# The head of a one-core encoder step in another order: smaller first loads, no GpSimd low parts, forms built between the steps of the first root

## The chip, the cores and the metric

One core of a Trainium2 chip runs the whole kernel. The metric is device time in microseconds (us) of one execution. The engines are named as in the profile: PE (TensorE matmul), PEld (its weight loads), DVE (VectorE), ACT (ScalarE), POOL (GpSimd) and SP (SyncE, which here only issues transfers).

## The reference, cut to what matters

One layer works on 576 time steps (512 of one stream, 64 of another) with 1024 features:

```python
x = x + 0.5 * swiglu_ffn(rms_norm(x, ffn1_norm), ffn1_w_gate_up, ffn1_w_down)
h = rms_norm(x, mix_norm); p = h @ w_in      # two gated convolution branches follow
...
x = x + 0.5 * swiglu_ffn(rms_norm(x, ffn2_norm), ffn2_w_gate_up, ffn2_w_down)

def rms_norm(x, g):
    return x * rsqrt(mean(x * x, -1) + EPS) * g
def swiglu_ffn(x, w_gate_up, w_down):
    gate, up = split(x @ w_gate_up, 2, -1)
    return (silu(gate) * up) @ w_down
```

Only the start of the first of these lines, the norm and the first columns of `ffn1_w_gate_up`, is touched by the change. Everything is float32.

## The kernel before, in words

**Numbers in two parts.** Features lie on the 128 partitions, the 576 steps in the free dimension, so x is eight tiles x0 to x7. A float32 product is made of three matmuls: each operand is a high part (a copy rounded to `fp32r`) and a low part (the rest), and high times high, high times low and low times high are added up in PSUM, for two halves of 288 columns, so six matmuls for each tile of 128 rows. The high part is always a copy on ACT (CAST, or ACTIVATE with a scale). The low part comes in one of three ways: a subtraction on DVE; a subtraction on POOL; or "by DMA", where ACT writes the negated high part and POOL issues a transfer that adds the source onto it (DMA_DIRECT2D on POOL, with `accum_op=add`).

**Order.** Every compute engine keeps the order in which the Python code issues its instructions (`keep_in_program_order`), so an instruction that waits holds up all that stand behind it on its engine. SP issues all loads in order. Raw weights go through a ring of six buffers of 128 x 512 (`wraw`, `RAWS = 6`): the seventh load waits until the first one has been used up, by its low part. `Stream.prep` does one weight unit: load, high part, low part; `weights()` does three units, one for each of the first three products (`FIRST`: gate column 0, up column 0, gate column 1).

**The head.** `load(j)` fetches x tile j, `begin(j)` makes its two parts scaled by the norm's gain (`split_scaled`: ACTIVATE on ACT, SCALAR_TENSOR_TENSOR on DVE), `squares(j)` squares it on ACT or POOL, and `ss.add(dve)` adds a square to the sum `acc`. The weights of the first three products come in units of 1, 3 and 4 tiles of 128 rows (`FIRST_KS`). PE takes the eight tiles one after the other, three products at a time (18 matmuls for a tile); before the eighth, `rstd` issues eight matmuls with a tile of ones that sum the squares over partitions. `rstd` then goes: DVE `a = sum/D + EPS`, ACT reciprocal root `r`, three DVE steps that refine it.

**Forms.** From column block 3 on, gate and up are computed together with seven products instead of eight (a Strassen-type scheme, `pair`). It needs sums of quarter tiles of scaled x, the forms. There are four pairs of x tiles, p = 0 to 3. `Forms.scale(p)` writes two scaled copies (`w<-x,gains`, ACT), `combine(p)` four DVE operations on halves (`tmp<-w`) into two tiles and their high parts on ACT, `split(p)` the two low parts, on DVE or (`by_dma=True`) by DMA.

**The first three column blocks** are plain: `plain(i)` issues the products gate i and up i, then

```python
            gate()      # DVE: t = gate * R;  ACT: t = Silu(t)
            forming()   # the next group of form steps of `todo`
            hidden()    # DVE: t = up * t;    ACT: high part of t
            parts()     # DVE: low part of t
            forming()
```

A product needs a PSUM tile of two banks, and there are four (`mmps`, `bufs=4`): gate 0, up 0, gate 1 and the sum of squares hold them first, then up 1, gate 2, up 2 and the first pair reuse them in that order. Up 1 therefore cannot start before DVE's `a`, gate 2 not before DVE's gate multiplication of block 0, up 2 not before the `hidden` multiplication of block 0, and the first pair not before the gate multiplication of block 1. In a row `tmp<-mm,r` is a gate multiplication and `tmp<-mm,tmp` (576 columns) a `hidden` one; `g`, `u` and `act` are tiles with high and low parts.

Of the kernel before, what the change touches and what calls it, by code (L numbers as in the profile page):

```python
# [43 lines left out]

HALVES = ((0, H), (H, T))
LATE_SPANS = (((0, 304),), ((304, T),))
FIRST_KS = (1, 3, 4)
WARM = 10


# [53 lines left out]
def tile_encoder_step(  # L104
# [7 lines left out]
    pe, dve, sca, pool = (  # L112
        Ordered(tc, e, c)
        for e, c in (
            (nc.tensor, pe_cost), (nc.vector, dve_cost), (nc.scalar, None), (nc.gpsimd, None)
        )
    )
# [12 lines left out]
    def nm(s):  # L130
        uid[0] += 1
        return f"{s}_{uid[0]}"

    def atile(dt=F32, n=T):
        return act.tile([P, T], dt, tag="act", name=nm("act"))[:, :n]
# [7 lines left out]
    def wtile(dt=F32, n=LB - HB):  # L143
        return conv.tile([P, LB - HB], dt, tag="w", name=nm("w"), bufs=6)[:, :n]

    def ttile(dt=F32):
        return tmp.tile([P, T], dt, tag="tmp", name=nm("tmp"))
# [16 lines left out]
    def half(ap, s):  # L164
        return ap[:, s * H : (s + 1) * H]
# [11 lines left out]
    X = [cpool.tile([P, T], F32, tag=f"x{j}", name=f"x{j}") for j in range(KT)]  # L177
# [15 lines left out]
    class Stream:  # L193
# [28 lines left out]
        def load(self, r):  # L222
            while len(self.loaded) <= r:
                ap, k = self.raws[len(self.loaded)]
                t = wraw.tile([P, KU, P], F32, tag="raw", name=nm("raw"))[:, :k, :]
                nc.sync.dma_start(t, ap)
                self.loaded.append(t)
# [16 lines left out]
        def add(self):  # L244

            _, k, _, _, sums = self.units[self.added]
            for name, ops in sums:
                v = wtile(n=k * P).rearrange("p (k n) -> p k n", n=P)
                a, b = (self.source(o) for o in ops)
                dve.tensor_tensor(v, a, b, op=ALU.add)  # L250
                self.sums[name] = v
            self.added += 1
            self.load_ahead()

        def begin(self):

            n = self.begun
            src, k, home, how, _ = self.units[n]
            v = self.source(src)
            make = {"u": utile, "g": gtile, "act": atile}[home]  # L260
            hi, lo = (make(F32R, k * P).rearrange("p (k n) -> p k n", n=P) for _ in range(2))
            sca.copy(hi, v)
            if how == "dma":

                sca.mul(lo, hi.bitcast(F32), -1.0)
                pool.dma_start(lo.bitcast(F32), v, accum_op=ALU.add)
            self.ready[n] = (hi, lo)
            self.begun += 1
            self.load_ahead()
# [93 lines left out]
    row = 0  # L363
    for k in FIRST_KS:
        for name in FIRST:
# [26 lines left out]
    def mm(ps, w, kk, xs, first, last, spans=HALVES):  # L392


        (whi, wlo), (xh, xl) = w, xs
        parts = ((whi, xh), (whi, xl), (wlo, xh))
        for n, s in SIX:
            if s < len(spans):
                (a, b), (i, e) = parts[n], spans[s]
                pe.matmul(  # L400
                    ps[:, s, : e - i], a[:, kk, :], b[:, i:e],
                    start=first and n == 0, stop=last and n == 2,
                )
# [59 lines left out]
    def high(v):  # L463
        hi = atile(F32R)
        sca.copy(hi, v)
        return hi
# [79 lines left out]
            n = spans[0][1] - spans[0][0]  # L546
            return p[:, :, :n] if len(spans) == 2 else p[:, 0, :n]

    def rstd(total, spans=HALVES):

        a, t = ttile(), ttile()
        r = rpool.tile([P, T], F32, tag="r", name=nm("r"), bufs=2)
        tot = total.total(spans)
        span = slice(spans[0][0], spans[-1][1])
        shaped = halves if len(spans) == 2 else (lambda v: v)
        a, t, y = a[:, span], t[:, span], r[:, span]
        dve.tensor_scalar(shaped(a), tot, 1.0 / D, EPS, op0=ALU.mult, op1=ALU.add)
        sca.activation(y, a, AF.Abs_reciprocal_sqrt)
        dve.scalar_tensor_tensor(t, y, -0.5, y, op0=ALU.mult, op1=ALU.mult)
        dve.tensor_tensor(t, t, a, op=ALU.mult)  # L560
        dve.scalar_tensor_tensor(y, t, 1.5, y, op0=ALU.add, op1=ALU.mult)
        return r


    class Forms:
# [9 lines left out]
                sca.activation(b, X[j], AF.Copy, scale=par(j, self.r_g))  # L575

        def combine(self, p):
            (b1, b2), (c, d) = self.b.pop(p), (ttile() for _ in range(2))
            for out, a, b, op in (
                (half(c, 0), half(b1, 0), half(b1, 1), ALU.subtract),  # L580
                (half(c, 1), half(b2, 1), half(c, 0), ALU.add),
                (half(d, 0), half(b1, 1), half(b2, 1), ALU.subtract),
                (half(d, 1), half(b2, 0), half(c, 1), ALU.subtract),
            ):
                dve.tensor_tensor(out, a, b, op=op)
            self.t[p] = [(v, high(v)) for v in (c, d)]

        def split(self, p, by_dma=False):
            self.parts[p] = [
# [12 lines left out]
            return first[:KU], t2, t1, t3, first[KU:], second[KU:], t4  # L602


    ss = Sum()
    xg = []
    def load(j):
# [5 lines left out]
    def weights(lo=dve):  # L613
        for _ in FIRST:
            ws.prep(lo)

    def squares(*js):
        for j in js:
            ss.square(X[j], pool if j in (0, 2, 4) else sca)

    load(0)
    begin(0)
    squares(0)
    weights()
    load(1)
    begin(1)
    weights()
    load(2)
    load(3)
    begin(2)  # L630
    begin(3)
    squares(1, 2)
    weights(pool)
    for j in range(4, KT):
        load(j)
    ss.add(dve)
    ss.add(dve)
    squares(3)
    begin(4)
    begin(5)  # L640
    ss.add(dve)
    squares(5, 4)
    ss.add(dve)
    ss.add(dve)
    begin(6)
    begin(7)
    squares(6, 7)
    ss.add(dve)
    ws.eager = True
    for _ in range(4):  # L650
        ws.prep()
    forms1 = Forms(R_N1)
    forms1.scale(0)
    forms1.scale(1)
    forms1.combine(0)
    nc.sync.dma_start(prm, prm_src[:, R_CA:, :])
    table(AF.Abs_reciprocal_sqrt)
    first = {name: psum2() for name in FIRST}
# [5 lines left out]
            firstw[name] += [(w, kk) for kk in range(ws.units[n][1])]  # L664
    for k in range(KT):
        if k == KT - 1:
            R1 = rstd(ss)
        for name in FIRST:
            w, kk = firstw[name][k]
            mm(first[name], w, kk, xg[k], k == 0, k == KT - 1)  # L670
# [2 lines left out]
    ps = product(name, xg)  # L673
    early[name] = ps


    def split_early(p):
        one.split(p, by_dma=True)

    def update(j, ps, R=None):  # L680

# [8 lines left out]
    def ffn(f, xg, sums, finish, forms, R=None, todo=()):  # L690
# [5 lines left out]
        def plain(i, hs):  # L696
# [4 lines left out]
            if R is None:  # L701
                R = rstd(sums)
# [105 lines left out]
    def finish1(g, hs):  # L808
        table(AF.Abs_reciprocal_sqrt)
        ps = both([("f1", "d", g, j) for j in range(2)], hs)  # L810
        for j in range(KT):
# [6 lines left out]
    one = forms1  # L818
    ffn(
        "f1", xg, ss, finish1, one, R1,  # L820
        (
            ((split_early, 0), (one.scale, 2), (one.combine, 1)),
            ((split_early, 1), (one.scale, 3), (one.combine, 2)),
            ((one.split, 2), (one.combine, 3)),
            ((one.split, 3),),
        ),
    )
    ss, xg = nss, nxg
# [92 lines left out]
    for j in range(KT):  # L921
        raw = j < RAW_J
        xs = xg if raw else xn
        product(("p", 4, j), xs, gate_b(j, raw))
        if R is None:
            R = rstd(ss)
        if raw:
            xn.extend(scaled(range(3 * j, min(KT, 3 * j + 3)), R))
        product(("p", 3, j), xs, value_b(j))
# [142 lines left out]
    ss = Sum()  # L1072
# [3 lines left out]
    for n, j in enumerate(IN_TURN):  # L1076
# [5 lines left out]
        p = n // 2  # L1082
# [114 lines left out]
```

## Time and profile before

| | us |
|---|---|
| runs, median (lowest to highest of 3) | 1302.98 (1302.82 to 1303.01) |
| the profiled execution's own time | 1303.07 |
| its span, first to last instruction | 1301.3 |
| PE busy in the span | 1286.3 (99%) |
| DVE, ACT, POOL busy | 892.0, 778.5, 400.5 |
| first matmul on data starts at | 5.29 |
| PE starts up 1, gate 2, up 2, first pair at | 29.06, 35.38, 41.70, 48.02 |

In a row of the timeline stand the start (us from the span's beginning), the time until its last instruction ends, the engine, the operation, what it writes and reads (`out<-in`, buffer numbers left out), the shape and the count; in brackets the idle time of the engine before it and what ended it. The granted PE clock was 0.998 over the span.

### The profile page before, as it was taken

How to read it: one execution, taken by the hardware profiler on the slowest of the kernel's cores; microseconds unless marked ns; L12 is line 12 of the kernel's file. 1: busy time of each engine (PE TensorE's matmuls, PEld its weight loads, DVE VectorE, ACT ScalarE, POOL GpSimd, SP SyncE). 2: the span in 40 equal slices, each digit the busy share in tenths (PEclk: the TensorE clock that was granted, in tenths of full speed). 3: DMA queues.
4: the chain of work that ended last, by engine and by line, in shares of the span. 5: the costliest groups of instructions: out<-in, count | busy, mean ns of one | idle time of the engine just before them, and what ended most of it. 6: DMA issues, size and time to landing. Idle time of an engine off the chain costs nothing.

```text
span 1301.3 us, 25714 instructions
## 1 busy us (share of the span) xinstructions
PE 1286.3 (99%) x9746; PEld 1282.5 (99%) x9746; DVE 892.0 (69%) x1460; ACT 778.5 (60%) x1374; POOL 400.5 (31%) x502
## 2 busy tenths in 40 slices
PE   9999999999999999999999999999999999999997
PEld 8999999999999999999999999999999999999996
DVE  6758758748945899888895260336967848847955
ACT  8755655645677655555554684457665655654664
POOL 4242332332242544322221322222142141241233
PEclk9999999999999999999999999999999999999999
DMA  9797787886798797877775978776687796796784
GB/s 245 141 189 160 148 185 157 165 192 147 152 195 182 167 216 173 175 166 170 172 168 125 199 158 178 154 166 142 138 169 165 162 192 149 163 206 136 161 178 107
DMA packets 290108, 218.40 MB, mean 168 GB/s; under 512 B 15680, under 2 KB 251200, under 8 KB 289984
## 3 DMA queue, kind: packets, MB, share of 16 engines
q0 software_dynamic: 60768, 100.30, 46.4%
q1 hardware_dynamic: 227488, 115.62, 31.4%
q8 instruction: 77, 1.26, 0.4%
q10 hardware_dynamic: 1728, 0.84, 0.2%
q14 instruction: 47, 0.39, 0.1%
HBM read 113.81 MB, written 2.62 MB: 89 GB/s over the span
## 4 chain that ended last, share of the span: by engine, by line
PE 90%; issue 4%; DMA 2%; ACT 1%; POOL 1%; DVE 1%; DVEq 0%; POOLq 0%; ACTq 0%; SPq 0%
PE mm L80 90%; DMA g<-raw 1%; DMA raw<-in_ffn_w_gate_up_dram 1%; POOL act L80 1%; DVE tmp L80 0%; ACT u L80 0%; DMA gains<-in_params_dram 0%; POOL g L80 0%; ACT tmp L80 0%; ACT g L80 0%; DVE acc L80 0%; ACT act L80 0%; DVE x L80 0%; DVE g L80 0%; POOL tmp L80 0%
## 5 line engine op out<-in xcount | busy, mean ns | idle before, releaser
L80 PE MATMUL mm<-act,u 128*128 128x288 f32 x4686 | 660.9, 294 | 0.7 <-DVE u L80 0.5
L80 PEld LDWEIGHTS mm<-act,u 128*128 128x128 f32 x4686 | 630.9, 188 | 1.2 <-DVE u L80 0.7
L80 PE MATMUL mm<-act,g 128*128 128x288 f32 x2766 | 398.6, 294 | 2.1 <-DMA g<-raw 2.0
L80 PEld LDWEIGHTS mm<-act,g 128*128 128x128 f32 x2766 | 376.5, 188 | 2.9 <-DMA g<-raw 2.8
L80 POOL DMA_DIRECT2D u<-raw x204 | 176.3, 864 | 550.4 <-ACT u L80 492.2
L80 PE MATMUL mm<-act,act 128*128 128x288 f32 (+2 forms) x2244 | 307.6, 293 | 1.4 <-DVE act L80 1.4
L80 PEld LDWEIGHTS mm<-act,act 128*128 128x128 f32 x2244 | 297.8, 188 | 2.4 <-DVE act L80 2.1
L80 POOL DMA_DIRECT2D g<-raw x124 | 108.6, 876 | 247.2 <-ACT g L80 188.2
L80 ACT CAST u<-raw 128x512 fp32r<-128x512 f32 (+2 forms) x204 | 117.1, 574 | 108.6 <-PE mm L80 76.5
L80 DVE SCALAR_TENSOR_TENSOR w<-g,prm,w 128x606 f32<-128x606 f32 x232 | 179.3, 844 | 1.4 <-ACT w L80 1.4
L80 DVE TENSOR_TENSOR tmp<-mm,tmp 128x288 f32<-128x288 f32 (+1 forms) x244 | 109.7, 458 | 72.9 <-PE mm L80 53.5
L80 ACT ACTIVATE u<-u 128x512 fp32r<-128x512 f32 (+2 forms) x204 | 121.1, 594 | 6.5
L80 POOL DMA_DIRECT2D act<-raw x90 | 78.9, 876 | 50.6 <-ACT act L80 49.5
L80 DVE SCALAR_TENSOR_TENSOR tmp<-mm,r 128x576 f32<-128x576 f32 x48 | 36.3, 757 | 78.0 <-PE mm L80 77.8
L80 ACT CAST g<-raw 128x512 fp32r<-128x512 f32 (+2 forms) x124 | 67.7, 546 | 35.3 <-DMA raw<-in_ffn_w_down_dram 14.7
L80 ACT CAST act<-tmp 128x576 fp32r<-128x576 f32 x84 | 56.2, 674 | 52.4 <-DVE tmp L80 51.6
L80 ACT CAST g<-w 128x512 fp32r<-128x512 f32 x80 | 49.6, 619 | 63.0 <-DVE w L80 56.6
L80 ACT CAST u<-w 128x512 fp32r<-128x512 f32 x80 | 49.5, 619 | 61.9 <-DVE w L80 55.7
L80 DVE TENSOR_TENSOR act<-tmp,act 128x576 fp32r<-128x576 f32 x80 | 59.3, 754 | 21.3 <-ACT act L80 19.8
L80 ACT ACTIVATE g<-g 128x512 fp32r<-128x512 f32 (+2 forms) x124 | 70.4, 568 | 3.9
L80 ACT CAST act<-raw 128x512 fp32r<-128x512 f32 (+2 forms) x99 | 57.6, 583 | 16.1 <-PE mm L80 11.0
L80 DVE TENSOR_TENSOR w<-raw,raw 128x512 f32<-128x512 f32 x80 | 54.8, 685 | 11.0 <-DMA raw<-in_ffn_w_gate_up_dram 11.0
(88 smaller groups left out, 814.1 us busy)
## 6 DMA issues: line engine op xcount, KB each, us to landing
raw<-in_ffn_w_gate_up_dram SPq DMA_DIRECT2D x173, 256.0 KB, 3.4
u<-raw POOLq DMA_DIRECT2D x145, 256.0 KB, 4.0
raw<-in_w_in_dram SPq DMA_DIRECT2D x112, 256.0 KB, 3.4
act<-raw POOLq DMA_DIRECT2D x80, 256.0 KB, 4.8
raw<-in_ffn_w_down_dram SPq DMA_DIRECT2D x96, 192.0 KB, 3.5
g<-raw POOLq DMA_DIRECT2D x65, 256.0 KB, 3.8
g<-raw POOLq DMA_DIRECT2D x43, 192.0 KB, 4.5
u<-raw POOLq DMA_DIRECT2D x43, 192.0 KB, 4.5
```

Source lines behind the costliest of these rows:

```text
L80: return self.tc.keep_in_program_order(fn(*args, **kwargs))
```

## The change

It has five parts. (1) The first weight units are 1, 1, 2 and 4 tiles instead of 1, 3 and 4. (2) The three low parts of the last unit are made by DVE instead of POOL; the square of x4 goes from POOL to ACT. (3) In the head's code the parts of x tiles (`begin`) are issued ahead of squares and additions. (4) `rstd` takes a function `meanwhile` that it calls behind the root on ACT: there the second form is added, and both forms 0 and 1 get their high parts and, by DMA, their low parts. Before, the form 0 was combined with its high parts ahead of the root, and the rest was done in `plain(0)`. (5) In `plain(0)` forms 2 and 3 are now done, with low parts by DMA; before, that was spread over `plain(0)` and `plain(1)`, and the low parts of 2 and 3 were DVE's.

```diff
-FIRST_KS = (1, 3, 4)
+FIRST_KS = (1, 1, 2, 4)
...
-    def rstd(total, spans=HALVES):
+    def rstd(total, spans=HALVES, meanwhile=None):
...
         sca.activation(y, a, AF.Abs_reciprocal_sqrt)
+        if meanwhile:
+            meanwhile()
         dve.scalar_tensor_tensor(t, y, -0.5, y, op0=ALU.mult, op1=ALU.mult)
...
         def combine(self, p):
+            self.add(p)
+            self.cast(p)
+
+        def add(self, p):
...
-            self.t[p] = [(v, high(v)) for v in (c, d)]
+            self.t[p] = c, d
+
+        def cast(self, p):
+            self.t[p] = [(v, high(v)) for v in self.t[p]]
...
+    def split_early(p):
+        forms1.split(p, by_dma=True)
...
-            ss.square(X[j], pool if j in (0, 2, 4) else sca)
+            ss.square(X[j], pool if j in (0, 2) else sca)
...
     load(2)
+    begin(2)
+    weights()
     load(3)
-    begin(2)
     begin(3)
-    squares(1, 2)
-    weights(pool)
+    weights()
     for j in range(4, KT):
         load(j)
-    ss.add(dve)
+    squares(1, 2)
+    begin(4)
     ss.add(dve)
     squares(3)
-    begin(4)
     begin(5)
-    ss.add(dve)
-    squares(5, 4)
     ss.add(dve)
     ss.add(dve)
     begin(6)
+    squares(4, 5)
     begin(7)
+    ss.add(dve)
     squares(6, 7)
+    ss.add(dve)
     ss.add(dve)
...
     forms1.scale(0)
+    forms1.add(0)
     forms1.scale(1)
-    forms1.combine(0)
...
         if k == KT - 1:
-            R1 = rstd(ss)
+            R1 = rstd(ss, meanwhile=lambda: (
+                forms1.add(1), forms1.cast(0), split_early(0), forms1.cast(1), split_early(1)
+            ))
...
-            ((split_early, 0), (one.scale, 2), (one.combine, 1)),
-            ((split_early, 1), (one.scale, 3), (one.combine, 2)),
-            ((one.split, 2), (one.combine, 3)),
-            ((one.split, 3),),
+            ((one.scale, 2), (one.combine, 2), (split_early, 2)),
+            ((one.scale, 3), (one.combine, 3), (split_early, 3)),
```

Three places of the built order matter below. The first is ACT between its last weight copy of the head (`act<-raw`) and the first copy for up 1 (`g<-raw`); `tmp<-x` are squares, `act<-x,gains` high parts of x tiles. Before:

```order
L80 CAST act_184<-raw_182 128x512
L80 ACTIVATE tmp_194<-x_91 128x576
L80 ACTIVATE act_196<-x_92,gains 128x576
L80 ACTIVATE act_200<-x_93,gains 128x576
L80 ACTIVATE tmp_205<-x_93 128x576
L80 ACTIVATE act_211<-x_94,gains 128x576
L80 ACTIVATE act_215<-x_95,gains 128x576
L80 ACTIVATE tmp_219<-x_94 128x576
L80 ACTIVATE tmp_221<-x_95 128x576
L80 CAST g_236<-raw_224 128x512
```

The same stretch of ACT now:

```order
L80 CAST act_198<-raw_196 128x512
L80 ACTIVATE tmp_206<-x_89 128x576
L80 ACTIVATE act_210<-x_92,gains 128x576
L80 ACTIVATE tmp_215<-x_91 128x576
L80 ACTIVATE act_217<-x_93,gains 128x576
L80 ACTIVATE act_223<-x_94,gains 128x576
L80 ACTIVATE tmp_227<-x_92 128x576
L80 ACTIVATE tmp_229<-x_93 128x576
L80 ACTIVATE act_231<-x_95,gains 128x576
L80 ACTIVATE tmp_236<-x_94 128x576
L80 ACTIVATE tmp_238<-x_95 128x576
L80 CAST g_254<-raw_242 128x512
```

Two more squares (x1, which stood ahead of this stretch, and x4, which was POOL's) are in it. The second place is ACT from the first scaled copies to the first unit of up 2 (`g_450` before, `g_490` now). Before:

```order
L80 ACTIVATE w_269<-x_93,gains 128x576
L80 CAST act_278<-tmp_272 128x576
L80 CAST act_280<-tmp_273 128x576
L80 ACT_TABLE_LOAD
L80 ACTIVATE table_283<-eps 128x1
L80 ACTIVATE r_416<-tmp_414 128x576
L80 CAST g_450<-raw_232 128x512
```

Now:

```order
L80 ACTIVATE w_293<-x_93,gains 128x576
L80 ACT_TABLE_LOAD
L80 ACTIVATE table_297<-eps 128x1
L80 ACTIVATE r_430<-tmp_428 128x576
L80 CAST act_444<-tmp_286 128x576
L80 CAST act_446<-tmp_287 128x576
L80 ACTIVATE act_448<-act_444 128x576
L80 ACTIVATE act_451<-act_446 128x576
L80 CAST act_454<-tmp_438 128x576
L80 CAST act_456<-tmp_439 128x576
L80 ACTIVATE act_458<-act_454 128x576
L80 ACTIVATE act_461<-act_456 128x576
```

Behind the last of these stands `g_490`: two copies have gone from ahead of the root `r` to behind it, and eight form operations now stand between the root and the weights of up 2. The third place is DVE between the gate multiplication of block 0 (`tmp<-mm,r`) and the low part of its hidden tile (`act<-tmp,act`). Before:

```order
L80 TENSOR_TENSOR tmp_521<-mm_285,r_416 128x576
L80 TENSOR_TENSOR tmp_534<-w_268 128x288
L80 TENSOR_TENSOR tmp_534<-w_269,tmp_534 128x288
L80 TENSOR_TENSOR tmp_535<-w_268,w_269 128x288
L80 TENSOR_TENSOR tmp_535<-w_269,tmp_534 128x288
L80 TENSOR_TENSOR tmp_521<-mm_286,tmp_521 128x576
L80 TENSOR_TENSOR act_547<-tmp_521,act_545 128x576
```

Now:

```order
L80 TENSOR_TENSOR tmp_561<-mm_299,r_430 128x576
L80 TENSOR_TENSOR tmp_568<-w_564 128x288
L80 TENSOR_TENSOR tmp_568<-w_565,tmp_568 128x288
L80 TENSOR_TENSOR tmp_569<-w_564,w_565 128x288
L80 TENSOR_TENSOR tmp_569<-w_565,tmp_568 128x288
L80 TENSOR_TENSOR tmp_561<-mm_300,tmp_561 128x576
L80 TENSOR_TENSOR act_587<-tmp_561,act_585 128x576
```

The rows look alike, but the four form operations read other copies: `w_268` and `w_269` were written ahead of the root, `w_564` and `w_565` are written by ACT behind the Silu of block 0.

More of the change, by code (lines that the diff above doesn't have):

```diff
@@ L674, in tile_encoder_step @@
     early[name] = ps
-    def split_early(p):
-        one.split(p, by_dma=True)
     def update(j, ps, R=None):
```

## The prediction

> **What bounds the kernel now.** The page gives PE as 99% busy, so I read busy time by stretches first, to see where anything but PE can matter.
>
> ```profile
> 5.30:29.00 23.70, 22.26 (x154) 20.99 (x154) 18.06 (x25) 21.35 (x36) 11.53 (x9) 1.00 1.04 268
> 29.00:76.00 47.00, 44.31 (x329) 43.28 (x327) 35.19 (x63) 35.70 (x63) 15.34 (x18) 1.00 0.75 149
> 76.00:1301.00 1225.00, 1215.43 (x9250) 1213.91 (x9248) 838.31 (x1373) 718.72 (x1271) 372.09 (x469) 1.00 0.78 167
> ```
>
> The columns are the stretch, its length, and busy time (count) of PE, PEld, DVE, ACT and POOL, then clock, DMA share and GB/s. Behind 76 us PE is never short of work for long, and the change does nothing there; the question is only when PE gets through the first 62 us. In the first stretch ACT is busy 21.35 of 23.70 us, more than DVE: ACT is the scarce engine of the head. Next the timeline of PE: where does it stand still?
>
> ```profile
> 11.60 0.66 PE L80 MATMUL mm<-act,act 128*128 128x288 f32 x3 [0.62 <-DVE act L80]
> 22.39 1.87 PE L80 MATMUL mm<-act,act 128*128 128x288 f32 x12 [0.82 <-DVE act L80]
> ...
> 29.06 3.19 PE L80 MATMUL mm<-act,g 128*128 128x288 f32 x23
> 35.38 3.32 PE L80 MATMUL mm<-act,g 128*128 128x288 f32 x24
> 41.70 3.32 PE L80 MATMUL mm<-act,g 128*128 128x288 f32 x24
> 48.02 1.74 PE L80 MATMUL mm<-act,g 128*128 128x288 f32 x12
> 49.60 1.49 PE L80 MATMUL mm<-act,u 128*128 128x288 f32 x10
> ...
> 60.84 1.60 PE L80 MATMUL mm<-act,g 128*128 128x288 f32 x10 [1.51 <-DMA g<-raw]
> 62.28 1.75 PE L80 MATMUL mm<-act,u 128*128 128x288 f32 x12
> ...
> 75.36 3.71 PE L80 MATMUL mm<-act,g 128*128 128x288 f32 x26 [0.47 <-DMA g<-raw]
> ```
>
> A product takes 6.32 us (29.06 to 35.38), a unit of the first pair 1.58 (48.02 to 49.60). PE waits 1.44 us in the head, and longest at 60.84, for the low part of the pair's seventh unit, which comes by DMA. So a head that PE passes sooner is worth something only if that low part comes sooner too. The chain of waits names its last steps, and the timeline of ACT shows what they hang on:
>
> ```profile
> 57.50 3.30 DMA g<-raw
> ```
> ```profile
> 13.20 0.62 ACT L80 CAST act<-raw 128x512 fp32r<-128x512 f32 x1 [0.24 <-DMA raw<-in_ffn_w_gate_up_dram]
> ...
> 17.56 1.25 ACT L80 ACTIVATE tmp<-x 128x576 f32<-128x576 f32 x2
> 18.71 0.61 ACT L80 CAST g<-raw 128x512 fp32r<-128x512 f32 x1
> ...
> 23.41 2.76 ACT L80 ACTIVATE w<-x,gains 128x576 f32<-128x576 f32 x4
> 26.07 1.23 ACT L80 CAST act<-tmp 128x576 fp32r<-128x576 f32 x2
> 27.32 1.28 ACT L80 ACT_TABLE_LOAD   x1
> ...
> 35.07 0.69 ACT L80 ACTIVATE tmp<-tmp 128x576 f32<-128x576 f32 x1
> 35.66 1.24 ACT L80 ACTIVATE act<-act 128x576 fp32r<-128x576 f32 x2
> 36.81 1.43 ACT L80 ACTIVATE w<-x,gains 128x576 f32<-128x576 f32 x2
> 38.14 1.81 ACT L80 CAST act<-tmp 128x576 fp32r<-128x576 f32 x3
> 39.85 1.26 ACT L80 ACTIVATE act<-act 128x576 fp32r<-128x576 f32 x2
> ...
> 45.53 0.69 ACT L80 ACTIVATE tmp<-tmp 128x576 f32<-128x576 f32 x1 [0.82 <-DVE tmp L80]
> 47.73 2.08 ACT L80 CAST act<-tmp 128x576 fp32r<-128x576 f32 x3 [1.51 <-DVE tmp L80]
> ...
> 53.84 0.69 ACT L80 ACTIVATE tmp<-tmp 128x576 f32<-128x576 f32 x1
> ```
>
> The rows without brackets followed the one before them without a wait: from 13.20 on, where ACT last waits for a load of the head, it is full for 30 us. The Silus of blocks 0, 1 and 2 (`tmp<-tmp`) stand at 35.07, 45.53 and 53.84, and the wanted low part lands 6.95 us after the third. I cost the change along this chain, in three sections.
>
> **ACT from 13.20 to the first Silu.** Two squares more (x1 and x4): two take from 17.56 to 18.71, +1.15. Two form copies less ahead of the root: 26.07 to 27.32, -1.25. Eight form operations more behind the root: a copy costs 0.57 (three from 38.14 to 39.85), a negated one 0.58 (35.66 to 36.81), so +4.6. Nothing covers them, since ACT has no gap to put them in. Sum +4.5: the first Silu at 39.6.
>
> **First to second Silu.** Both now have 15 ACT operations between them, but the waits differ. The DVE rows for it, before:
>
> ```profile
> 44.74 0.75 DVE L80 TENSOR_TENSOR tmp<-mm,r 128x576 f32<-128x576 f32 x1
> ...
> 47.23 0.46 DVE L80 TENSOR_TENSOR tmp<-w,tmp 128x288 f32<-128x288 f32 x1
> ...
> 48.35 0.75 DVE L80 TENSOR_TENSOR tmp<-mm,tmp 128x576 f32<-128x576 f32 x1
> 49.84 2.10 DVE L80 TENSOR_TENSOR act<-tmp,act 128x576 fp32r<-128x576 f32 x3 [0.74 <-ACT act L80]
> 51.85 0.69 DVE L80 TENSOR_TENSOR u<-w,u 128x512 fp32r<-128x512 f32 x1
> 52.45 0.69 DVE L80 TENSOR_TENSOR w<-w,raw 128x512 f32<-128x512 f32 x1
> ```
>
> Silu at 39.6, 0.59 to the next operation, two scaled copies 1.43: 41.6. Only then can DVE do the last three form operations of p = 2 (47.23 to 48.35: 1.12) and the hidden multiplication behind them (0.75): 43.5. On ACT the second form's high part waits for the fourth form operation and ends at 43.5, two negated copies and the hidden high part (0.67) end at 45.2, two scaled copies at 46.6. DVE's three operations for p = 3 end at 47.8, then a high part, two negated copies and the g copy on ACT: 50.2; DVE's low part of g (0.6 until the next starts, as from 51.85 to 52.45) and the gate multiplication of block 1 (0.75): 51.6. The second Silu moves from 45.53 to 51.6, so this section is 12.0 instead of 10.46: +1.55.
>
> **Second to third Silu.** Here the change pays back: no forms and no form low parts stand in this section any more. Silu 0.69, hidden multiplication 0.75, its high part 0.67, its low part 0.67, the low part and sum of weights 0.6 each, gate multiplication 0.75, and 0.04 at four handovers: 4.9 instead of 8.31, -3.4. From there to the landing nothing changes, 6.95.
>
> **The sum:** 4.5 + 1.55 - 3.4 = +2.65. The low part lands at 63.45 instead of 60.79, the seventh unit ends as much later, and 1303.07 becomes 1305.7. That is against the profiled execution; the median of the runs is 0.09 lower, so I say 1305.6.
>
> **PE on the way.** Smaller loads, DVE low parts instead of these,
>
> ```profile
> 12.49 5.16 POOL L80 TENSOR_TENSOR act<-raw,act 128x512 fp32r<-128x512 f32 x3 [1.55 <-ACT act L80]
> ```
>
> and inputs ahead of squares can free at most the 1.44 us of head waits and the restarts beside them. But up 1 needs the bank that DVE's `a` frees, and `a` stands behind form 0, which needs the second scaled copy: 23.41 + 1.43 + 1.15 = 26.0, three form operations 1.2, `a` 0.75: 28.0 against 29.06, a gain of 1.1 at most. Gate 2 then starts at 34.3 and up 2 could at 40.6, but its bank is freed at 43.5: a new wait of 2.9 us. It ends at 49.8, and the first pair's bank is free at 51.6: another 1.8. The pair's seven units (11.06) then end at 62.65 without any further wait, at 64.9 with the late low part, against 62.28 now. So the head's gain is covered by a wait behind it, whatever its size: I cost parts 1 to 3 at nothing, as long as PE reaches up 2 before 43.5. The wait at 51.3 for DVE's low part of form 3 goes with that operation; what is late in its place is the bank. The four more form transfers on POOL's queue stand ahead of the last two g and u transfers, but POOL idles more than it works (15.34 of 47.00 us), so I take nothing; at most they crowd the last landing, whose median over the kernel is longer than the 3.30 here:
>
> ```profile
> g<-raw POOLq DMA_DIRECT2D x65, 256.0 KB, 3.8
> ```
>
> That bounds it at 0.5 us more; below 3.3 I see none. The wait at 75.36 (0.47 and a restart) moves along, since ACT, DVE and PE shift alike; if it is absorbed, 0.7 comes back.
>
> **The start of the chain.** Where ACT's 13.20 goes is not shown before: the third load of the four-tile unit is issued later. Before, the three were issued one behind the other from 5.87:
>
> ```profile
> 5.87 1.48 SPq L226 DMA_DIRECT2D raw<-in_ffn_w_gate_up_dram  x3
> ```
> ```profile
> 7.16 0.82 DVE L80 SCALAR_TENSOR_TENSOR act<-x,gains,act 128x576 fp32r<-128x576 f32 x1 [0.92 <-ACT act L80]
> ```
>
> Now their buffers are those of tile 1's unit, freed by the DVE low parts that follow x1's (the second row) from 7.9 on, so SP issues the third at about 9.2 instead of 6.9. From issue to landing the loads took:
>
> ```profile
> DMA to landing us min/median/max: 2.7/3.7/4.1
> ```
> ```profile
> DMA to landing us min/median/max: 5.5/6.0/6.3
> ```
>
> The first row is of the six loads up to 5 us, the second of the three after it, in a full queue. So it lands between 11.9 and 15.5, and ACT can be held up by +2.3; below, the copies of x3 and the two loads ahead of it keep ACT busy until about 12.6, so -0.6. I take no shift: the DMA share of 1.04 says the engines move bytes without pause in this stretch, and the bytes ahead of this load are the same as before. The Trainium skill ("DMA: Bandwidth & Descriptors", section "Bandwidth") speaks against the smaller loads: it gives 0.95 us of transfer for 64 KB and 6.15 for 1 MB, and advises batches of 1 MiB. By its table, interpolated, three loads of 64 and three of 128 KB take about 6.7 us where three of 192 KB take 4.9; an estimate by that page would put the sum at 1307.4. The rows before show loads overlapping, so I give that no more than the rival below.
>
> **Rivals.** (a) *The chain starts sooner.* If ACT's load comes 0.6 earlier and the wait at 75.36 is absorbed as well, 2.65 falls to 1.35: 1304.3, not slower by what can be told. From 0.1 us saved on it decides, since 0.2% is 2.6. For it: nothing ties the load to 13.20. Against: the same bytes precede it, and both savings are needed for the full amount. Chance 0.22. (b) *The smaller loads arrive late:* ACT starts up to 2.3 us later and each microsecond goes to the end, 1307 in the middle, 1308 at most. Against it stands the full DMA share. Chance 0.13. (c) *The head's gain stays:* up 1's 1.1 us with all other waits unchanged gives 1301.9, and with the pair's wait of 1.5 gone too 1300.4. It needs the first Silu by about 36.7 (2.9 earlier than I put it), so ACT would have to hide five of the eight operations; the rows show no gap. Chance 0.08. (d) *All is covered, no change,* 1303: the four low parts that DVE drops (2.7 us) would have to shorten the chain by 2.65 more than I count in the third section, where I already let two of them go. Chance 0.05. My forecast, 1305.6 with 1304.9 to 1306.4 as its own range, has 0.52.
>
> **Numbers.** A measurement here tells 0.2% (2.6 us) from no change. Slower by more: a little over half of my forecast, 0.3, and nearly all of (b): 0.42. Faster by more is half of (c): 0.04. Same: 0.54. The range 1302.5 to 1307.2 leaves out (c) and the far half of (b), and 0.05 around them.
>
> **What would show it.** After: PE waiting about 3 us before up 2 (near 43) and about 1.8 before the pair (near 51), each for a DVE `tmp`; the Silus near 39.6, 51.6 and 56.5; the seventh unit's low part landing near 63.4; no wait for DVE's `act` in the pair. I am wrong if ACT has a gap between 13 and 40, if its start at 13.20 moves by over 0.6, or if a PE wait of the pair is set by another landing.

## The result, and the profile after

The changed kernel takes 1307.63 us (median of 6 runs, 1306.55 to 1308.62) beside 1302.93 us for the kernel before on the same chip. The ratio is 1.0035, with a 95% interval of 1.0024 to 1.0045: slower by 0.35%, about 4.7 us, where +2.6 was forecast. The profiled execution took 1307.66 us with a span of 1305.9, 4.6 longer than before.

Where the time goes is read in the same order as before. First the stretches (length, busy time of PE, PEld, DVE, ACT and POOL with counts, clock, DMA share, GB/s):

```profile
5.30:29.00 23.70, 22.49 (x154) 21.28 (x153) 16.85 (x31) 20.06 (x36) 4.74 (x5) 1.00 0.94 244
29.00:76.00 47.00, 41.39 (x303) 40.27 (x304) 30.77 (x56) 38.73 (x68) 16.71 (x20) 1.00 0.85 171
76.00:1301.00 1225.00, 1218.71 (x9273) 1216.74 (x9272) 839.24 (x1376) 719.41 (x1275) 375.62 (x471) 1.00 0.79 167
```

The loss is in the second row: PE got through 303 matmuls from 29 to 76 us, against 329 before. ACT has become busier there (38.73 us, 35.70 before). The first row holds something unforecast: the DMA share fell from 1.04 to 0.94. Next, the rows of PE's timeline in which it stood still:

```profile
29.30 3.40 PE L80 MATMUL mm<-act,g 128*128 128x288 f32 x24 [0.47 <-DVE tmp L80]
36.30 3.46 PE L80 MATMUL mm<-act,g 128*128 128x288 f32 x24 [0.43 <-DVE tmp L80]
44.69 3.36 PE L80 MATMUL mm<-act,g 128*128 128x288 f32 x24 [1.70 <-ACT act L80]
52.91 1.82 PE L80 MATMUL mm<-act,g 128*128 128x288 f32 x12 [1.75 <-DVE tmp L80]
60.30 1.59 PE L80 MATMUL mm<-act,g 128*128 128x288 f32 x10 [0.55 <-DMA g<-raw]
64.64 1.60 PE L80 MATMUL mm<-act,g 128*128 128x288 f32 x10 [0.88 <-DMA g<-raw]
```

The two forecast waits are there, 1.70 us before up 2 and 1.75 before the first pair, and the pair still ends on its seventh unit, whose low part comes by DMA. The row at 44.69 names ACT, but the forecast cause fits: DVE's multiplication that frees the bank of up 2 ends at 44.54 (43.79 + 0.75).

```profile
43.79 0.75 DVE L80 TENSOR_TENSOR tmp<-mm,tmp 128x576 f32<-128x576 f32 x1
```

The old wait at 51.3 for a low part by DVE is gone. The wait of 0.55 us at 60.30 is new: it is for an earlier low part of the pair, also by DMA, and one of the signs that the prediction named for being wrong. Up 1 starts at 29.30, no sooner than before (29.06). Last, the chain on ACT, and the chain of waits where it ends:

```profile
12.77 0.62 ACT L80 CAST act<-raw 128x512 fp32r<-128x512 f32 x1 [0.39 <-DMA raw<-in_ffn_w_gate_up_dram]
13.65 0.62 ACT L80 CAST act<-raw 128x512 fp32r<-128x512 f32 x1 [0.26 <-DMA raw<-in_ffn_w_gate_up_dram]
14.47 0.62 ACT L80 CAST act<-raw 128x512 fp32r<-128x512 f32 x1 [0.20 <-DMA raw<-in_ffn_w_gate_up_dram]
...
40.62 0.69 ACT L80 ACTIVATE tmp<-tmp 128x576 f32<-128x576 f32 x1
...
52.80 0.68 ACT L80 ACTIVATE tmp<-tmp 128x576 f32<-128x576 f32 x1 [0.91 <-DVE tmp L80]
...
57.68 0.69 ACT L80 ACTIVATE tmp<-tmp 128x576 f32<-128x576 f32 x1
```
```profile
61.34 3.26 DMA g<-raw
```

The last weight copy of the head starts at 14.47 instead of 13.20, the Silus at 40.62, 52.80 and 57.68, and the low part lands at 64.60 (61.34 + 3.26) instead of 60.79: 3.81 us later. Of this lag 0.35 us is made up by 143 us (PE is 3.46 behind there); about 0.25 is lost near 346 us and 0.56 near 942, and the last matmul starts 4.27 later than before. The last 0.3 us of the span come behind it.

### The profile page after: what moved, and what is told of

It reads as the page before. It is cut to its first block, busy times and chain, and to the rows that moved or that the text cites. A ratio compares the mean times of both kernels' runs of the same rounds, so it can differ in the third digit from the quotient of the medians.

```text
span 1305.9 us, 25749 instructions
## 1 busy us (share of the span) xinstructions
PE 1286.9 (99%) x9746; PEld 1282.6 (98%) x9746; DVE 888.0 (68%) x1462; ACT 780.9 (60%) x1382; POOL 398.7 (31%) x502
## 3 DMA queue, kind: packets, MB, share of 16 engines
q8 instruction: 77, 1.26, 0.4%
## 4 chain that ended last, share of the span: by engine, by line
PE 89%; issue 4%; ACT 3%; DMA 2%; DVE 1%; POOL 0%; SPq 0%; DVEq 0%; POOLq 0%; ACTq 0%
PE mm L80 89%; DMA g<-raw 1%; ACT act L80 1%; DVE tmp L80 1%; DMA raw<-in_ffn_w_gate_up_dram 1%; ACT u L80 1%; ACT tmp L80 1%; ACT g L80 0%; ACT w L80 0%; DVE acc L80 0%; SPq L226 0%; POOL g L80 0%; DVE x L80 0%; DVE g L80 0%; POOL act L80 0%
## 5 line engine op out<-in xcount | busy, mean ns | idle before, releaser
L80 DVE TENSOR_TENSOR act<-tmp,act 128x576 fp32r<-128x576 f32 x76 | 56.6, 754 | 19.7 <-ACT act L80 18.3
L80 ACT CAST act<-raw 128x512 fp32r<-128x512 f32 (+3 forms) x102 | 58.1, 571 | 16.5 <-PE mm L80 11.0
L80 DVE TENSOR_TENSOR w<-raw,raw 128x512 f32<-128x512 f32 x80 | 54.8, 686 | 12.1 <-DMA raw<-in_ffn_w_gate_up_dram 12.1
```

The lines of the kernel that those rows point to most:

```text
L80: return self.tc.keep_in_program_order(fn(*args, **kwargs))
```

## The experiments

Each kernel ran beside the kernel before on the same chip. "Copy" is the start of ACT's last weight copy of the head, "landing" that of the first pair's last low part, both from one profiled execution, while the median is of all runs; the share is that of the DMA engines from 5 to 11 us. Kernels are in the order of the landing.

| kernel | share | copy | landing | median us | ratio (95%) |
|---|---|---|---|---|---|
| e9: combination, root first | 0.99 | 13.12 | 59.83 | 1303.14 | 0.9999 to 1.0022 |
| before | 1.06 | 13.20 | 60.79 | 1303 | 1 |
| e7: head only, two squares on DVE | 1.02 | 13.01 | 60.84 | 1303.35 | 0.9994 to 1.0011 |
| e6: e7 and four low parts by DVE | 0.98 | 13.01 | 61.34 | 1304.80 | 1.0011 to 1.0038 |
| e10: before, small loads only | 0.87 | 13.75 | 61.58 | 1304.07 | 0.9999 to 1.0016 |
| e3: before, forms moved only | 1.04 | 13.07 | 62.12 | 1304.55 | 1.0001 to 1.0019 |
| e5: head only | 1.02 | 13.67 | 62.92 | 1305.03 | 1.0005 to 1.0023 |
| e1: after, units of 1, 3, 4 | 1.04 | 13.17 | 63.24 | 1305.39 | 1.0011 to 1.0028 |
| e2: after, forms as before | 0.83 | 14.43 | 63.77 | 1305.70 | 1.0012 to 1.0030 |
| e4: after, own buffers | 0.90 | 13.69 | 63.80 | 1306.99 | 1.0018 to 1.0041 |
| e13: after, loads joined | 1.01 | 14.18 | 64.35 | 1306.08 | 1.0013 to 1.0031 |
| e16: e1, loads cut | 0.91 | 14.35 | 64.44 | 1306.58 | 1.0017 to 1.0039 |
| e12: after, x3 first, own buffers | 0.88 | 14.43 | 64.55 | 1306.72 | 1.0017 to 1.0039 |
| e11: after, x3 first | 0.89 | 14.45 | 64.59 | 1306.81 | 1.0017 to 1.0039 |
| after | 0.80 | 14.47 | 64.60 | 1307.63 | 1.0024 to 1.0045 |

Above 60.8 the time follows the landing roughly one to one (e4, e6 and the changed kernel itself are about 1 us above that); below it, in e9, it doesn't. The medians of e6 and e9 stand for two groups of times each, see the last section.

### One part alone, and one part undone

**e3**, only parts 4 and 5: the head and `FIRST_KS` are those before.

```diff
-FIRST_KS = (1, 1, 2, 4)
+FIRST_KS = (1, 3, 4)      # and load ... squares ... add of the head as before
```

> The kernel before with only the forms moved (parts 4 and 5 of the change); its head as before. Theory: ACT to the first Silu -1.25 + 4.6 = +3.35, to the second +1.55, to the third -3.4: the low part lands at 60.79 + 1.5 = 62.3, time 1304.5. Rival (the forms carry the whole loss): 1307.6. Rival (moving them is neutral, the loss is the head's): 1303.0.

Time 1304.55, landing 62.12, against 1304.5 and 62.3. From the copy at 13.07, the Silus stand at

```profile
38.19 0.69 ACT L80 ACTIVATE tmp<-tmp 128x576 f32<-128x576 f32 x1
50.31 0.68 ACT L80 ACTIVATE tmp<-tmp 128x576 f32<-128x576 f32 x1 [0.91 <-DVE tmp L80]
...
55.18 0.69 ACT L80 ACTIVATE tmp<-tmp 128x576 f32<-128x576 f32 x1
```

so the sections are 25.1, 12.1 and 4.9 us (before: 21.9, 10.5, 8.3), and the forms' share of the loss is 1.3 us at the landing. Neither rival holds: the forms alone are not the whole loss, and moving them isn't neutral.

**e2**, the forms put back and the head left changed:

```diff
+    forms1.combine(0)
...
-            R1 = rstd(ss, meanwhile=...)
+            R1 = rstd(ss)      # and todo of plain as before
```

> The changed kernel with the forms where they were before (form 0 ahead of the root, the rest in the plain blocks, low parts of forms 2 and 3 by DVE); the head as changed. Theory (one chain on ACT, every microsecond of the head goes through): the first Silu at 35.07 + 1.27 (late loads) + 1.15 (two squares) = 37.5, the low part lands at 60.79 + 2.4 = 63.2, time 1305.4. Rival (the forms carry the whole loss and the head's delay is taken up by waits): 1303.0 to 1303.5.

1305.70 and a landing at 63.77, 0.3 and 0.6 above the theory; the rival (1303.0 to 1303.5) is out. ACT's timeline shows the excess, a wait for the first raw load of the first pair (the third weight copy behind the root; up 2's two stand ahead of it), which the kernel before hardly had (0.14 us):

```profile
34.95 0.62 ACT L80 CAST g<-raw 128x512 fp32r<-128x512 f32 x1 [0.82 <-DMA raw<-in_ffn_w_gate_up_dram]
```

**e1**, the units back at 1, 3 and 4 tiles:

```diff
-FIRST_KS = (1, 1, 2, 4)
+FIRST_KS = (1, 3, 4)
     begin(2)
-    weights()
     load(3)
```

> The changed kernel with the weight units of the head back at 1, 3 and 4 tiles; all else as changed. Theory (the late start of ACT's chain is the smaller units' doing, worth 1.27 of the 3.81 us by which the pair's seventh low part lands later): ACT's last weight copy of the head starts near 13.2 instead of 14.47, the low part lands near 63.3 instead of 64.6, time near 1306.3. Rival (the order of loads and x parts in the head delays it, not the sizes): the copy stays near 14.4 and the time at 1307.6. Rival (the late loads explain the whole loss): 1303.

Copy at 13.17 and landing at 63.24, as the theory has it; the time came out at 1305.39, 0.9 below the theory. So the change without its small units still loses 2.4 us, and with them about 2.2 more in the medians, 1.36 of it at the landing.

**e10**, the small units alone on the kernel before:

```diff
-FIRST_KS = (1, 3, 4)
+FIRST_KS = (1, 1, 2, 4)
     begin(2)
+    weights()
     begin(3)
```

> The kernel before with only its weight units at 1, 1, 2 and 4 tiles (part 1 alone). Theory: the third four-tile load is issued near 9 and lands near 14.4, ACT's last weight copy starts 1.2 us later than in the kernel before, all later ACT work with it, so the last low part lands at 62.0 and the time is 1304.2. Rival (the late load costs only together with the new order of the head): 1303.0. Rival (an improvement, since smaller loads let PE start sooner): 1302.

1304.07 and a landing at 61.58, near the theory. But the copy started only 0.55 us later (13.75), not the 1.2 expected, though the third four-tile load was issued at 8.96, as expected. The interval (0.9999 to 1.0016) doesn't separate it from no change, and with 0.07% it is the smallest part. It isn't faster.

### Is the head's earlier pass worth anything?

**e5** keeps of the change only parts 2 and 3 (loads of 1, 3 and 4 tiles, forms as before); **e7** also moves the squares of x1 and x4 from ACT to DVE:

```diff
-            ss.square(X[j], pool if j in (0, 2) else sca)
+            ss.square(X[j], {0: pool, 1: dve, 2: pool, 4: dve}.get(j, sca))
```

> The changed kernel with loads of 1, 3 and 4 tiles and the forms where they were before: what is left of the change is the head's order, the low parts by DVE instead of GpSimd, and the squares of x1 and x4 on ACT behind the last weight copy. Theory (ACT's chain): chain starts near 13.2 as before, two squares more, so the low part lands at 60.79 + 1.15 = 61.9 and the time is 1304.1, although PE passes the head about 1 us sooner. Rival (PE's earlier head is worth something by itself): 1302.

> As the head-only kernel (loads of 1, 3 and 4 tiles, forms as before, low parts by DVE), with the squares of x1 and x4 on DVE instead of ACT. Theory: ACT's chain is as long as before, so the low part lands near 60.8 and the time is 1303.0, with PE's start of up 1 about 1 us earlier all the same and all of that lost again at the waits. Rival (the head's earlier pass counts): 1302. Rival (DVE now is late with the sum of squares): 1304.

e5 took 1305.03, 0.9 above the theory: its landing at 62.92 is +0.47 by a later copy, +1.15 by the squares, and about the rest a wait of 0.71 us (0.14 before) for the same raw load as in e2 (at 34.09). e7 took 1303.35, ratio 1.0003: no change. Its PE timeline is the clearest evidence of the study:

```profile
27.86 3.32 PE L80 MATMUL mm<-act,g 128*128 128x288 f32 x24
...
46.81 1.74 PE L80 MATMUL mm<-act,g 128*128 128x288 f32 x12
...
51.36 0.53 PE L80 MATMUL mm<-act,u 128*128 128x288 f32 x2 [1.48 <-DVE act L80]
...
60.89 1.60 PE L80 MATMUL mm<-act,g 128*128 128x288 f32 x10 [1.52 <-DMA g<-raw]
```

PE starts up 1 at 27.86 instead of 29.06 and is 1.21 us ahead at the first pair (46.81 against 48.02). At 51.36 it waits for DVE's low part of a form, 1.48 instead of 0.23 us, and at 60.89 it is 0.05 behind the kernel before. The whole 1.2 us is handed back, because ACT's chain did not move.

### What makes the chain start late?

Four kernels change how the loads of the head are asked for. **e4** gives the six one-tile loads buffers of their own (`g` tiles), so that SP need not wait until DVE has freed the ring; **e8** also issues three of these from ACT near the program's start (ahead of the first x copy, with the copy of the ones moved behind them); **e11** issues x3's load ahead of the two-tile loads; **e12** is e4 and e11 together.

```diff
+                if k == 1:                                   # e4, e8, e12
+                    t = gtile(n=P).rearrange("p (k n) -> p k n", n=P)
...
-                nc.sync.dma_start(t, ap)                     # e8
+                (sca if len(self.loaded) in (3, 4, 5) else nc.sync).dma_start(t, ap)
...
     load(2)
+    load(3)                                                  # e11, e12
     begin(2)
     weights()
-    load(3)
```

> The changed kernel with the six one-tile loads of the head in buffers of their own, so that no later load of the head waits for DVE to free the ring; same bytes, same sizes, same order of issue. Theory (the third four-tile load is late because it is issued 2.2 us later, behind DVE's low parts): it is issued before 8, ACT's last weight copy starts near 13.2 and the time falls by 1.3 to 1306.3. Rival (small loads use the queue worse, so the bytes themselves come later): the copy stays at 14.2 to 14.5 and the time at 1307.6.

> The changed kernel with buffers of their own for the six one-tile loads, and the second three of them issued by ACT at the program's start instead of by SP. It tells what holds the last 0.5 us of the late start. Theory (SP needs about 0.5 us for each issue, so small loads come in slower than the engines could carry them): the third four-tile load is issued near 6.5 instead of 8.0 and ACT's last weight copy starts at 13.2 or sooner instead of 13.69. Rival (small loads are slower to carry, or the bytes alone set it): the copy stays near 13.7.

> The changed kernel with the load of x3 issued ahead of the two-tile weight loads instead of behind them. From 5 to 11 us the DMA engines were busy 0.80 of the time in the changed kernel against 1.06 before, and 0.87 with the smaller loads in the old order, where x3 fills the time in which the two-tile loads wait for their buffers. Theory (the late start is bytes that were not asked for in time: 0.55 us by the ring, 0.7 by x3 standing behind the waiting loads): ACT's last weight copy starts near 13.75 instead of 14.47, the last low part lands near 63.9 instead of 64.60, time 1306.9. Rival (x3's place is without effect, or x3 first delays the weights): the copy at 14.4 or later, 1307.6.

> Both together: x3's load first, and buffers of their own for the one-tile loads, so that SP never waits for DVE while the queue has room; sizes still 1, 1, 2 and 4 tiles. Theory (asked for in time, the same bytes land as before whatever the sizes): DMA share from 5 to 11 us near 1, the last copy starts at 13.0 to 13.3, the last low part lands near 63.4, time 1306.3. Rival (the sizes themselves cost about half a microsecond): the copy stays at 13.7.

e4 looked like a part success of the ring theory (third four-tile load issued at 8.00, copy at 13.69 instead of 14.47; but 1306.99, between the theory and its rival). e11 and e12 speak against it, and against x3's place as the cause. In e11 the copy stayed at 14.45, as its rival has it, though the time of 1306.81 is nearer the theory. In e12 SP no longer waited for the ring, the third load was issued at 8.31, and the copy still came at 14.43, later than both the theory (13.0 to 13.3) and the rival (13.7); the share was 0.88, not near 1. e8 is inconclusive: SP issued nothing between 2.6 and 3.9 us there, ACT its third load only at 4.13, and the third four-tile load went out at 8.30, not 6.5; the copy was at 13.66, as the rival has it, the time 1307.35 in its one run. So the next four asked whether the loads themselves, their number and size, do it, and how far executions differ. **e13** keeps units of 1, 1, 2 and 4 tiles but fetches the second and third by one load of three tiles; **e16** is e1 with each of its three-tile loads cut into one and two tiles; **e14** and **e15** are the changed kernel and e4 again.

```diff
+    for k, cuts in ((1, ((0, 1),)), (3, ((0, 1), (1, 3))), (4, ((0, 4),))):          # e13
+        rs = [ws.raw(ffn1_gu, row, k, gu_col(*name[1:])) for name in FIRST]
...
+                cuts = (0, 1, 3) if len(self.loaded) in (3, 4, 5) else (0, k)       # e16
+                for a, b in zip(cuts, cuts[1:]):
+                    nc.sync.dma_start(t[:, a:b, :], ap[:, a:b, :])
```

> The changed kernel with its units of 1, 1, 2 and 4 tiles, but the second and third unit of a product fetched by one load of three tiles (six loads become three). Theory (count and size of the loads: SP issues one in about 0.48 us, so small loads ask for the same bytes later and the queue runs short of work from 5 to 9 us): DMA share from 5 to 7 us back near 1.0, last weight copy near 13.1, last low part near 63.3, time 1305.4 as with loads and units of 1, 3 and 4. Rival (the finer units hold it): the copy stays at 13.7 to 14.5 and the time at 1307.

> The changed kernel with units of 1, 3 and 4 tiles (which had the copy at 13.17 and 1305.4 us), but each of the three loads of three tiles cut in two, of one and two tiles: same units and buffers, three loads more. Theory (count and size of the loads): DMA share from 5 to 7 us falls to about 0.75, the copy moves to between 13.7 and 14.5, and the time rises by 0.5 to 1.3. Rival (finer units, not loads): the copy stays at 13.1 to 13.2 and the time at 1305.4.

> The changed kernel once more, for the spread of the start of ACT's chain between executions. If the start is set by the order of issue alone, the copy is at 14.4 to 14.5 again; if executions differ by themselves, it can be at 13.7.

> The changed kernel with buffers of their own for the six one-tile loads once more, which had the copy at 13.69. If the ring's wait is worth 0.75, it is at 13.7 again; if executions differ by themselves, it can be at 14.4.

The stretch from 5 to 11 us, in this order: before, after, e1, e16, e13. The last two numbers are DMA share and GB/s.

```profile
5.00:11.00 6.00, 5.97 (x40) 5.59 (x39) 3.92 (x9) 3.92 (x8) 1.16 (x2) 1.00 1.06 321
```
```profile
5.00:11.00 6.00, 6.00 (x40) 5.90 (x40) 4.16 (x11) 3.56 (x10) 1.15 (x1) 1.00 0.80 233
```
```profile
5.00:11.00 6.00, 5.85 (x40) 5.22 (x39) 3.91 (x9) 4.03 (x8) 1.15 (x1) 1.00 1.04 315
```
```profile
5.00:11.00 6.00, 5.79 (x39) 5.39 (x38) 3.68 (x8) 3.17 (x7) 0.42 (x2) 1.00 0.91 260
```
```profile
5.00:11.00 6.00, 5.57 (x38) 5.11 (x38) 2.72 (x8) 2.29 (x7) 0.20 (x1) 1.00 1.01 303
```

e16 differs from e1 in nothing but the cut of three loads, and all that was expected of it came: the share falls from 1.04 to 0.91, the copy moves from 13.17 to 14.35 (first row e1, second e16) and the median from 1305.39 (11 runs, 1304.82 to 1306.47) to 1306.58 (7 runs on another chip, 1306.09 to 1308.03; the kernel before took 1303.00 and 1303.13 beside them).

```profile
13.17 0.62 ACT L80 CAST act<-raw 128x512 fp32r<-128x512 f32 x1 [0.21 <-DMA raw<-in_ffn_w_gate_up_dram]
```
```profile
14.35 0.62 ACT L80 CAST act<-raw 128x512 fp32r<-128x512 f32 x1 [0.24 <-DMA raw<-in_ffn_w_gate_up_dram]
```

e13 joins the loads again, which also shortens the wait for the ring and brings the two-tile bytes ahead of x2. The share returns to 1.01 as expected; the rest was missed: the copy at 14.18, the landing at 64.35 and 1306.08 instead of 13.1, 63.3 and 1305.4. That copy is the third of this row:

```profile
13.03 1.77 ACT L80 CAST act<-raw 128x512 fp32r<-128x512 f32 x3
```

ACT was late there already, after waits of 1.26 and 1.20 us for three-tile loads (at 8.41 and 9.92), and the last load landed only at 14.16, though it was issued at 6.76, as in e1 (6.80, landed at 13.14). So a full share alone doesn't place the copy, and e13 doesn't rule out its rival, that finer units add to the delay. Over all kernels the share is 0.98 to 1.06 with loads of three tiles (eight executions) and 0.80 to 0.91 with the small ones issued by SP alone (nine). That is shown: small loads leave the DMA engines partly without work there. The likely reason is the cost of an issue on SP. Three issues took as long for loads of 192 KB before (first row) as for loads of 64 KB after (second row):

```profile
3.07 1.50 SPq L226 DMA_DIRECT2D raw<-in_ffn_w_gate_up_dram  x3
```
```profile
3.07 1.39 SPq L226 DMA_DIRECT2D raw<-in_ffn_w_gate_up_dram  x3
```

At one load in 0.48 us, SP can ask for at most 137 GB/s with loads of 64 KB and 273 with 128 KB, below the 321 GB/s that the kernel before moved; with 192 KB, at 0.50 us, it is 393 (estimates from these rows). Three more loads of 0.48 us ask for the same bytes 1.4 us later. The copy's exact start is not settled by it: with large loads it was 13.01 to 13.67 in seven executions and 14.18 in e13; with small ones issued by SP 14.35 to 15.62 in seven and 13.69 and 13.75 in two. The changed kernel alone gave 14.47 and, again, 15.62 (1308.01 in that run); e4 gave 13.69 and then 14.39 (1307.07). A single execution can't rank the kernels with small loads among each other, and e4's gain of 0.8 can't be told from this spread.

### A version that beats both?

**e6** takes e7 and makes the low parts of up 1's and gate 2's four weight units on DVE, which takes four negated copies off ACT. **e9** is e6 with form 0 added behind `a` and its high parts made behind the root.

```diff
+            how = "dve" if name in (("f1", "u", 1), ("f1", "g", 2)) else "dma"      # e6, e9
+            plan[name].append(ws.unit(r, k, home_of or home(other), how))
...
-    forms1.combine(0)                                                               # e9
...
-            R1 = rstd(ss)
+            R1 = rstd(ss, meanwhile=lambda: forms1.combine(0))
```

> As the kernel with the two squares on DVE, and the low parts of the four weight units of up 1 and gate 2 by DVE instead of by DMA: ACT loses four negated copies (0.63 each), 2.5 us, ahead of the root. Theory (each microsecond off ACT's chain comes sooner at the last low part): it lands near 58.3 to 59.0, the pair's 1.5 us wait goes, and the time is 1300.6 to 1301.5, faster than the kernel before. Rival (another wait takes its place at once: DVE's four more low parts of 0.6, or the raw loads): 1303.

> The combined kernel (loads of 1, 3 and 4 tiles, squares of x1 and x4 on DVE, four weight low parts by DVE) with form 0 added on DVE behind the sum's step a, and its two high parts on ACT behind the root, so that the root waits for no form. In the combined kernel ACT stood idle 2.7 us for form 0. Theory: the root starts near 26.4 instead of 29.27, the first Silu near 33.2 instead of 35.61 (35.07 before), the last low part lands near 58.9 (60.79 before), time 1301.1, faster than the kernel before by 1.9. Rival (DVE, now fuller, or the raw loads of up 2 hold the Silu where it was): 1303 to 1304.

e6 was no faster: the low part landed at 61.34, not at 58.3 to 59.0. DVE's additional work held up form 0, and ACT waited for it ahead of the root:

```profile
26.43 1.41 ACT L80 CAST act<-tmp 128x576 fp32r<-128x576 f32 x2 [2.70 <-DVE tmp L80]
```

The 2.5 us taken off ACT turned into 2.7 us of waiting. e9 removes most of that wait (1.10 us are left, for DVE's `a`): root at 26.33, first Silu at 34.02 instead of 35.07 (33.2 expected), landing at 59.83, 0.96 us sooner (58.9 expected). Its median is 1303.14, the same as before, and not 1301.1. In the profiled execution PE is 0.97 us ahead until 350 us and as much behind at the end; one place is the wait near 942 us, and about as much is lost between 1200 and 1290:

```profile
937.79 1.60 PE L80 MATMUL mm<-act,g 128*128 128x288 f32 x10 [0.73 <-DMA g<-raw]
```

Nothing here beats the kernel before measurably.

## Why the prediction was wrong

**The bound was right.** The chain on ACT, and not PE's way through the head, sets the end of the first pair. The table's landing and time move together over a range of 3.8 us, and e7 shows the opposite case, an earlier PE that gains nothing.

**The three sections were right.** From copy to first Silu the changed kernel took 26.15 us (forecast 39.6 - 13.2 = 26.4), then 12.18 (12.0) and 4.88 (4.9); then 6.92 to the landing (6.95). Their sum at the landing is +2.54, against +2.65 forecast. ACT has no gap from 14.47 to 42, as the prediction says. e3 confirmed the forms' part of it alone, and e7 against e5 that two squares on ACT are on the path (landings 2.08 us apart, of which 0.66 is e5's later copy).

**The failed step is "I take no shift"**, the start of the chain. It was costed at 0 with bounds of -0.6 and +2.3; it measured +1.27 in the profiled execution, and +2.42 in the other one of the same kernel (e14), both over the 0.6 that it named as a sign of being wrong. The late issue itself was forecast rightly, at about 9.2 (9.05 measured). The reason for no shift was that a DMA share of 1.04 means that the engines move bytes without pause, and that the bytes ahead are the same. The bytes are the same, but the share of the kernel before was no property of the head: it depended on loads of 192 KB, and fell to 0.80 with the smaller ones; and even with a share of 1.01 the last load landed 1.0 us later in e13 than in e1. What rival (b) described happened, with a price near its middle, and 0.13 was too low a chance. How large the shift is varies between executions, and that part of the cause is open. The Trainium skill ("DMA: Bandwidth & Descriptors", section "Bandwidth") gave the right direction: the estimate by its table was 1307.4, and the DMA shares here agree that small loads carry less. Its table is of transfers issued from GpSimd, while SP issues these, and no run here times a load alone.

**The rest** is 0.8 us of the 4.6 in the span. Near 942 us the changed kernel has a wait; the kernel before shows none there, only a unit that takes 2.17 us (at 937.19) instead of 1.75:

```profile
942.02 1.60 PE L80 MATMUL mm<-act,g 128*128 128x288 f32 x10 [0.70 <-DMA g<-raw]
```

Across this place PE's lag changed by -0.4 to +0.8 us in the kernels above, with no link to their edit (+0.56 after, -0.42 in e11, +0.62 in e12). So I take it as a difference between executions; that the median shows as much as the profile is not explained by it, and stays open. "PE on the way" was right in kind: waits of 1.70 and 1.75 (2.9 and 1.8 forecast), the first smaller because up 1 had not gained its 1.1 us and gate 2 waited another 0.43. Up 1 lost its gain by the same failed step: the forecast start of 28.0 and the shift of 1.27 give 29.3, where it stood. Crowding by the four more form transfers was rightly left out: the last transfer took 3.26 us (3.30 before), though the g and u transfers behind the first forms took up to 7.09.

Of the whole loss, the parts alone cost 0.9 us (small loads, e10), 1.8 (head's order, e5) and 1.5 (forms, e3) in the medians, 4.2 to 4.3 together; measured together, 4.7. (e10's share alone can't be told from nothing.)

## What to carry to other kernels

Find the chain that sets when the next unhidden transfer is issued, and cost an edit by what it adds to that chain's engine; PE's gains ahead of it are returned at the next wait. A full DMA queue under one size of load says nothing of another size: when loads are split, count the issues on the queue's engine and ask whether each brings enough bytes for the time that it takes. Work moved between two engines that alternate, as ACT and DVE do here, only helps if the other one is not waited for in the same chain.

## What was not expected

PE can fall behind at full clock without a wait that the profile shows. In e6's profiled execution it got through 4270 matmuls from 369 to 930 us, busy all the time by its rows; the kernel before (second row) got through 4308:

```profile
369.00:930.00 561.00, 561.00 (x4270) 561.00 (x4269) 366.36 (x553) 326.34 (x532) 173.84 (x242) 1.00 0.79 167
```
```profile
369.00:930.00 561.00, 561.00 (x4308) 561.00 (x4308) 371.95 (x564) 329.63 (x538) 175.00 (x243) 1.00 0.79 169
```

That is 0.9% fewer. The runs of e6 and e9 fall into two groups: e6 has seven from 1303.59 to 1304.93 and five from 1309.69 to 1310.62, e9 eight from 1302.00 to 1304.03 and four from 1307.53 to 1308.88, while the other kernels stay within 3.4 us. The profile of e6 is of its upper group and that of e9 of its lower one, so whether all of the upper runs lose their time in this way is not shown. Both kernels make four weight low parts of the head on DVE; why that matters hundreds of microseconds later is open.

GpSimd's low parts had slowed DVE: before, two low parts of x tiles took 3.15 us on DVE (from 15.11) while POOL subtracted; without that they take 0.82 and 0.81 (at 15.08 and 16.48 in e1). e3 and e10, where POOL subtracts too, have 3.18 and 3.36. That gain is real and lies off the path.
